# Two products of a hybrid decoder trunk by Strassen's seven-product scheme, with a new table of durations for the instruction planner

## The chip, the cores and the metric

The kernel runs on one core of one Trainium2 chip. The metric is the device time of one execution in microseconds (us), taken as the median of three runs. The profile is of one execution, recorded by the hardware profiler. TensorE is written PE (its weight loads PEld), VectorE is DVE, ScalarE is ACT, GpSimd is POOL, and SyncE, which issues all the transfers here, is SP.

## The reference

Two layers work on 512 tokens of 1024 features, all in float32:

```
h = h + concat(sparse_attention_heads, mlstm_heads) @ w_out      # "mix"
u = rms_norm(h, g_mlp) @ w_ff1                                   # 1024 -> 4096
h = h + square(relu(u)) @ w_ff2                                  # 4096 -> 1024
gate = sigmoid(rms_norm(h, g_ple) @ w_ple_gate + b_ple_gate)     # 1024 -> 1024
h = h + gate * (p_i @ w_ple)
```

The two products that the change touches are the one with `w_ff1` ("ff1") and the one with `w_ple_gate` ("gate").

## The kernel before

**Layout.** The residual stream `h` stays in SBUF as 8 feature blocks of 128 partitions by 512 tokens. A float32 product is made of three passes of float32r matmuls: both operands are split into a leading part `hi` and a remainder `lo`, and `hi*hi`, `hi*lo` and `lo*hi` are added up in one PSUM bank (`mm3`). A weight tile is 128 x 1024 (512 KB). It is loaded into `raw`, ACT writes `hi`, and DVE (in one place POOL may) writes `lo = raw - hi` (`weight`). The block `k` of `h` is scaled by the norm's gain and split by `split_block` in `prep`; POOL adds up the squares for the norm, and `wide_r` turns them into one factor for each token, which is applied to the products' results.

**Order of the MLP.** An output block of ff1 is 8 feature blocks times three passes, 24 matmuls of 128 x 512. `act` takes it out of PSUM with relu and the norm's factor (`s_v`), squares it (`hi` by ACT, `s_vv` by DVE or POOL, and the remainder by DVE). Nine blocks of ff1 stand ahead, then 8 blocks of ff2 (24 matmuls each, added to `h`) and 8 of ff1 take turns, four times in all, the last with no ff1 left. `ple` follows with 8 gate blocks. Two small products of 24 matmuls for the per-layer input (`inputs`, label `filler`) are held for free places on PE.

**What sets the order.** No loop order reaches the chip directly. `Plan` records every instruction, and `schedule` is a list scheduler: an idle engine at once takes the ready instruction with the longest chain of work behind it, using the durations in `cost` and the hops in `lag`. An instruction recorded in forms for two engines goes to the one that takes it first; the engines are asked in the order DVE, ACT, POOL, PE, SP. `issue` writes the result out, so on the chip every engine works through a fixed list. Within a chain (`nc.chain = "mlp"`) the matmuls keep the order in which they were recorded. Buffers come from rooms with a limited number of places (`ROOMS`): 3 for `raw`, 4 for `hi`, 4 for `lo`, 60 for 128 x 512 tiles (`s`), and 6 PSUM banks for products.

All instructions carry the line of `issue` (L381) in the profile, so one goes by tile names.

## Time and profile before

| | |
|---|---|
| time, median of 3 runs | 1372.2 us (1370.88 to 1372.2) |
| the profiled execution's span | 1370.7 us |
| PE busy | 1333.6 us (97%) |
| DVE busy | 887.2 us (65%) |
| ACT busy | 554.8 us (40%) |
| POOL busy | 188.1 us (14%) |
| HBM traffic | 84 GB/s over the span |

The span runs from the first to the last instruction of one execution; the median of the runs shown lies 1.5 us above it, and no other time of the profiled execution itself is given. Busy shares are averages over stages that differ: in the first layer the MLP runs from some 284 to 635 us, and the gate stage, with its two neighbours at the seams, to some 697 us.

### The profile page before, as it was taken

What the parts mean: (1) busy time and instruction counts of PE and PEld (TensorE: products, weight loads), DVE (VectorE), ACT (ScalarE), POOL (GpSimd) and SP (SyncE); (2) the same over time, 40 slices, a digit from 0 to 9 for tenths busy, and PEclk for the clock granted to TensorE, in tenths of its full rate; (3) what the DMA queues carried; (4) which work ended last, traced back from release to release, by engine and by line L of the source; (5) the groups of instructions that cost most, each with busy time, mean ns of one, the idle gap of its engine ahead of it and who ended that gap; (6) DMA issues with size and microseconds to landing.
All of it is one profiled execution on the core that took longest, in us unless ns stands there. A gap on an engine that the chain in (4) does not pass through costs nothing.

```text
span 1370.7 us, 17012 instructions
## 1 busy us (share of the span) xinstructions
PE 1333.6 (97%) x6336; PEld 1096.2 (80%) x6336; DVE 887.2 (65%) x1791; ACT 554.8 (40%) x1106; POOL 188.1 (14%) x151
## 2 busy tenths in 40 slices
PE   7979999999999999999998899999999999999998
PEld 6767889888888888888896778988888888888887
DVE  7989998575354453554859999966743534535454
ACT  4765486332122221234546644844222212222441
POOL 4244200120000000012104341003100000000210
PEclk9989999999999999999999899999999999999999
DMA  5212211333333233333231123103223233323321
GB/s 189 70 55 78 92 32 32 93 92 92 96 95 101 93 92 92 93 100 96 80 90 50 66 83 93 32 21 102 93 93 93 93 97 99 97 93 92 95 83 69
DMA packets 34355, 116.40 MB, mean 85 GB/s; under 512 B 4192, under 2 KB 4704, under 8 KB 34272
## 3 DMA queue, kind: packets, MB, share of 16 engines
q1 hardware_dynamic: 34272, 115.32, 27.4%
q8 instruction: 49, 0.80, 0.2%
q14 instruction: 34, 0.28, 0.1%
HBM read 113.21 MB, written 2.10 MB: 84 GB/s over the span
## 4 chain that ended last, share of the span: by engine, by line
PE 88%; DVE 8%; ACT 2%; issue 1%; DMA 1%; POOL 0%; SPq 0%; ACTq 0%; DVEq 0%; POOLq 0%
PE ps_proj L381 78%; PE ps_sc L381 3%; PE ps_tr L381 3%; DVE s L381 3%; PE ps_po L381 2%; PE ps_pn L381 1%; ACT s L381 1%; DVE s_w L381 1%; DVE wide L381 1%; DVE s_sp L381 1%; DVE m L381 1%; DVE tiny L381 1%; DVE lo L381 0%; POOL s L381 0%; DMA raw<-wa 0%
## 5 line engine op out<-in xcount | busy, mean ns | idle before, releaser
L381 PE MATMUL ps_proj<-s,hi 128*128 128x512 f32 x2960 | 920.1, 393 | 0.4 <-ACT hi L381 0.4
L381 PEld LDWEIGHTS ps_proj<-s,hi 128*128 128x128 f32 x2960 | 554.3, 188 | 127.0 <-issue 1.8
L381 PE MATMUL ps_proj<-s,lo 128*128 128x512 f32 (+1 forms) x1480 | 576.9, 393 | 0.3 <-DVE lo L381 0.3
L381 ACT ACTIVATE hi<-raw 128x1024 fp32r<-128x1024 f32 (+1 forms) x212 | 222.4, 1052 | 646.2 <-PE ps_proj L381 317.3
L381 PEld LDWEIGHTS ps_proj<-s,lo 128*128 128x128 f32 x1480 | 278.2, 188 | 64.1 <-DVE lo L381 0.7
L381 DVE TENSOR_TENSOR lo<-raw,hi 128x1024 fp32r<-128x1024 f32 (+1 forms) x181 | 223.2, 1234 | 33.9 <-ACT hi L381 30.9
L381 DVE TENSOR_TENSOR const<-const,ps_proj 128x512 f32<-128x512 f32 x96 | 66.0, 688 | 224.3 <-PE ps_proj L381 224.3
L381 POOL TENSOR_TENSOR lo<-raw,hi 128x1024 fp32r<-128x1024 f32 x31 | 75.6, 2442 | 531.9 <-ACT hi L381 525.0
L381 DVE SCALAR_TENSOR_TENSOR s_v<-ps_proj,s 128x512 f32<-128x512 f32 x64 | 43.9, 691 | 138.3 <-PE ps_proj L381 138.3
L381 POOL TENSOR_TENSOR s<-s,s 128x512 f32<-128x512 f32 x42 | 68.3, 1626 | 411.5 <-ACT s L381 297.0
L381 PE MATMUL ps_proj<-hi,s 128*128 128x512 f32 (+1 forms) x384 | 112.4, 381 | 7.2 <-ACT hi L381 7.2
L381 PE MATMUL ps_sc<-s,s 128*128 128x384 f32 (+3 forms) x288 | 85.4, 382 | 0.0
L381 PEld LDWEIGHTS ps_proj<-hi,s 128*128 128x128 f32 x384 | 69.3, 194 | 16.3 <-ACT hi L381 7.2
L381 PE MATMUL ps_proj<-lo,s 128*128 128x512 f32 (+1 forms) x192 | 66.5, 385 | 1.9 <-DVE lo L381 1.9
L381 PEld LDWEIGHTS ps_sc<-s,s 128*128 128x128 f32 x288 | 52.5, 195 | 9.4 <-issue 3.1
L381 ACT ACTIVATE s<-ps_tr 128x128 fp32r<-128x128 f32 (+2 forms) x170 | 38.9, 307 | 34.4 <-PE ps_tr L381 34.1
L381 DVE MATCH_REPLACE8 s<-m,s 128x384 f32<-128x384 f32 (+2 forms) x96 | 51.2, 537 | 0.0
L381 DVE TENSOR_TENSOR s<-s_vv,s 128x512 fp32r<-128x512 f32 x64 | 49.2, 773 | 0.2
L381 PE MATMUL ps_po<-at,s_et 128*128 128x64 f32 x320 | 48.9, 254 | 0.0
L381 DVE MAX8 m<-s 128x8 f32<-128x384 f32 (+2 forms) x96 | 48.8, 542 | 0.0
L381 PEld LDWEIGHTS ps_po<-at,s_et 128*128 128x128 f32 x320 | 47.8, 191 | 1.1
L381 DVE SCALAR_TENSOR_TENSOR s<-const,const,s 128x512 fp32r<-128x512 f32 x48 | 39.8, 833 | 11.5 <-ACT s L381 11.4
(133 smaller groups left out, 1105.0 us busy)
## 6 DMA issues: line engine op xcount, KB each, us to landing
raw<-ws SPq DMA_DIRECT2D x204, 512.0 KB, 3.5
raw<-wa SPq DMA_DIRECT2D x8, 336.0 KB, 3.4
const<-xt SPq DMA_DIRECT2D x8, 256.0 KB, 4.7
out<-const SPq DMA_DIRECT2D x7, 256.0 KB, 2.0
s<-pt SPq DMA_DIRECT2D x4, 256.0 KB, 4.1
const<-ct SPq DMA_DIRECT2D x2, 132.0 KB, 4.2
out<-const SPq DMA_DIRECT2D x2, 128.0 KB, 1.7
const<-cf SPq DMA_DIRECT2D x2, 39.0 KB, 2.7
```

The lines of the kernel that those rows point to most:

```text
L381: ins = getattr(getattr(nc, e), method)(*[value(x) for x in args], **{k: value(x) for k, x in kw.items()}).ins
```

## The change

ff1 and the gate product are made by the Winograd form of Strassen's scheme. Two output blocks (rows), the even and odd feature blocks (the inner dimension) and the two halves of the tokens (columns) make a 2 x 2 by 2 x 2 block product, which takes seven block products in place of eight. Each of the seven is 4 feature blocks times three passes of 128 x 256 matmuls. The operands are sums and differences: `seven` makes T1 to T4 from `h` once for each stage, `left` makes S1 to S4 from two weight tiles for every pair of output blocks, and `pair` lets the products add up in three PSUM banks and combines what is left on ACT and DVE. `interleaved` records the products of a pair between those of its neighbour. The host orders the rows of both weights even blocks first (`even_first`), with no other arithmetic there.

Besides, ten blocks of ff1 stand ahead of ff2 where nine did; the first two blocks of ff2 run together, with their last two feature blocks last; the tiles `at` and `vx` become four tiles each in the room `s`, which grows from 60 to 64 places, and `raw` grows from 3 to 4; and `cost` has other numbers.

```diff
             if method == "transpose":
-                return 56.0 if single else 109.0
-            return max(107.0, n / 2.4 + 3) if single else max(214.0, n / 0.6 + 3)
+                return 60.0 if single else 109.0
+            return max(111.0, n * 0.4375 + 7) if single else max(172.0, n * 1.66 + 11)
...
-            return 100 + n * {"tensor_tensor": 2.25, "memset": 0.5, "affine_select": 1.0}.get(method, 1.4)
+            return 100 + n * {"tensor_tensor": 2.4, "memset": 0.8, "affine_select": 1.0}.get(method, 1.4)
...
+    def quads(self, l, gcol):
+        nc = self.nc
+        label = nc.label
+        cf = self.cf[l][0]
+        H = S // 2
+        lower, upper = slice(0, H), slice(H, S)
+        xs, acc = [], None
+        for k in range(KD):
+            nc.label = "prep"
+            x = self.slot([128, S])
+            g = cf[:, gcol + k:gcol + k + 1]
+            nc.scalar.activation(x, self.h[k], AF.Copy, scale=g)
+            nc.label = "squares"
+            sq = self.slot([128, S])
+            nc.scalar.activation(sq, self.h[k], AF.Square)
+            if acc is None:
+                acc = sq
+            else:
+                nacc = self.slot([128, S])
+                nc.gpsimd.tensor_tensor(nacc, acc, sq, op=ALU.add)
+                acc = nacc
+            if k % 2 == 0:
+                b1 = x
+                continue
+            b2 = x
+            nc.label = "prep"
+            xs.append(self.seven(b1, b2))
+        nc.label = label
+        return xs, acc
+    def seven(self, b1, b2):
+        H = S // 2
+        lower, upper = slice(0, H), slice(H, S)
+        t12, t34 = self.slot([128, S]), self.slot([128, S])
+        self.either(t12[:, lower], b1[:, upper], b1[:, lower], ALU.subtract)
+        self.either(t34[:, lower], b2[:, upper], b1[:, upper], ALU.subtract)
+        self.either(t12[:, upper], b2[:, upper], t12[:, lower], ALU.subtract)
+        self.either(t34[:, upper], b2[:, lower], t12[:, upper], ALU.subtract)
+        out = {}
+        mixed = self.slot([128, S], F32R)
+        self.split(b1[:, lower], mixed[:, lower], mixed[:, upper])
+        out["B11"] = (mixed[:, lower], mixed[:, upper])
+        for names, src in ((("B21", "B22"), b2), (("T1", "T2"), t12), (("T3", "T4"), t34)):
+            hi, lo = self.slot([128, S], F32R), self.slot([128, S], F32R)
+            self.split(src, hi, lo)
+            out[names[0]], out[names[1]] = (hi[:, lower], lo[:, lower]), (hi[:, upper], lo[:, upper])
+        return out
+    def either(self, out, a, b, op):
+        nc = self.nc
+        return nc.add([(e, "tensor_tensor", (out, a, b), {"op": op}) for e in ("vector", "gpsimd")])
+    def split(self, src, hi, lo):
+        nc = self.nc
+        nc.scalar.activation(hi, src, AF.Copy)
+        nc.vector.tensor_tensor(lo, src, hi.bitcast(F32), op=ALU.subtract)
+    def left(self, l, i):
+        nc = self.nc
+        a, b = slice(0, 512), slice(512, 1024)
+        r1, r2 = self.slot([128, 1024], F32, "raw"), self.slot([128, 1024], F32, "raw")
+        nc.sync.dma_start(r1, self.ap["ws"][l, i])
+        nc.sync.dma_start(r2, self.ap["ws"][l, i + 1])
+        out = {}
+        def halves(src, names):
+            hi, lo = self.slot([128, 1024], F32R, "hi"), self.slot([128, 1024], F32R, "lo")
+            self.split(src, hi, lo)
+            for name, c in zip(names, (a, b)):
+                out[name] = (hi[:, c], lo[:, c])
+        halves(r1, ("A11", "A12"))
+        s1 = self.slot([128, 512])
+        self.either(s1, r2[:, a], r2[:, b], ALU.add)
+        hi, lo = self.slot([128, 512], F32R), self.slot([128, 512], F32R)
+        self.split(s1, hi, lo)
+        out["S1"] = (hi, lo)
+        self.either(r2[:, a], r1[:, a], r2[:, a], ALU.subtract)
+        self.either(r1[:, a], s1, r1[:, a], ALU.subtract)
+        self.either(r1[:, b], r1[:, b], r1[:, a], ALU.subtract)
+        halves(r1, ("S2", "S4"))
+        halves(r2, ("S3", "A22"))
+        return out
+    def pair(self, l, i, xs, take):
+        nc = self.nc
+        H = S // 2
+        lower, upper = slice(0, H), slice(H, S)
+        w = self.left(l, i)
+        def product(bank, left, right, first=False):
+            steps = [(k, a, b) for k in range(len(xs)) for a, b in ((0, 0), (0, 1), (1, 0))]
+            for n, (k, a, b) in enumerate(steps):
+                nc.tensor.matmul(bank[:, 0:H], w[left][a][:, k * 128:(k + 1) * 128], xs[k][right][b],
+                                 start=first and n == 0, stop=n == len(steps) - 1, skip_group_check=True)
+        u0, u1 = self.slot([128, S]), self.slot([128, S])
+        x, z = self.psum("proj"), self.psum("proj")
+        product(z, "A12", "B21", True)
+        nc.scalar.activation(u0[:, lower], z[:, 0:H], AF.Copy)
+        product(x, "A11", "B11", True)
+        nc.vector.tensor_tensor(u0[:, lower], u0[:, lower], x[:, 0:H], op=ALU.add)
+        yield
+        y = self.psum("proj")
+        product(y, "S1", "T1", True)
+        nc.scalar.activation(u1[:, upper], y[:, 0:H], AF.Copy)
+        product(x, "S2", "T2")
+        nc.scalar.activation(u0[:, upper], x[:, 0:H], AF.Copy)
+        yield
+        product(x, "S3", "T3")
+        nc.vector.tensor_tensor(u1[:, upper], u1[:, upper], x[:, 0:H], op=ALU.add)
+        yield
+        product(y, "S4", "B22")
+        nc.vector.tensor_tensor(u0[:, upper], u0[:, upper], y[:, 0:H], op=ALU.add)
+        product(x, "A22", "T4")
+        take(0, u0, u1, x)
+        yield
+    def interleaved(self, parts):
+        last = None
+        for p in parts:
+            next(p)
+            if last:
+                next(last)
+            next(p)
+            if last:
+                next(last)
+            last = p
+        next(last)
+        next(last)
...
+    def blocks(self, ws, xs, t=slice(0, S), late=1):
         pss = [self.psum("proj") for _ in ws]
-        steps = [(i, k) for i in range(len(ws)) for k in range(KD - 1)] + [(i, KD - 1) for i in range(len(ws))]
+        early = KD - late
+        steps = [(i, k) for i in range(len(ws)) for k in range(early)] \
+            + [(i, k) for i in range(len(ws)) for k in range(early, KD)]
...
-        xs, acc = self.prep(l, C_MLP)
+        xs, acc = self.quads(l, C_MLP)
...
...
+        H = S // 2
+        lower, upper = slice(0, H), slice(H, S)
+        def act(i):
+            def take(n, u0, u1, x):
+                if "r" not in state:
+                    state["r"] = self.wide_r(acc, D)
+                r = state["r"]
+                nc.vector.scalar_tensor_tensor(u0, u0, 0.0, r, op0=ALU.max, op1=ALU.mult)
+                nc.vector.scalar_tensor_tensor(u1[:, lower], x[:, 0:H], 0.0, r[:, lower], op0=ALU.max, op1=ALU.mult)
+                nc.vector.scalar_tensor_tensor(u1[:, upper], u1[:, upper], 0.0, r[:, upper], op0=ALU.max, op1=ALU.mult)
+                for j, v in ((i, u0), (i + 1, u1)):
+                    hi, lo = self.slot([128, S], F32R), self.slot([128, S], F32R)
+                    nc.scalar.activation(hi, v, AF.Square)
+                    self.either(v, v, v, ALU.mult)
+                    nc.vector.tensor_tensor(lo, v, hi.bitcast(F32), op=ALU.subtract)
+                    fs[j] = (hi, lo)
+            return take
+        def ff1(i, n):
+            self.interleaved(self.pair(l, W_FF1 + j, xs, act(j)) for j in range(i, i + n, 2))
         def ff2(c):
-            for n in range(KD):
-                ps, = self.blocks([self.wtile(l, W_FF2 + KD * c + n)], [fs[KD * c + k] for k in range(KD)])
-                nc.vector.tensor_tensor(self.h[n], self.h[n], ps, op=ALU.add)
-                if c == NFF - 1 and n == 0:
+            for n0, cnt in ((0, 2),) + tuple((n, 1) for n in range(2, KD)):
+                ws = [self.wtile(l, W_FF2 + KD * c + n0 + j) for j in range(cnt)]
+                pss = self.blocks(ws, [fs[KD * c + k] for k in range(KD)], late=2)
+                for n, ps in enumerate(pss, n0):
+                    nc.vector.tensor_tensor(self.h[n], self.h[n], ps, op=ALU.add)
+                if c == NFF - 1 and n0 == 0:
                     nc.hold, nc.chain = nc.ops[-1], None
                     self.inputs(l, 1, raws)
                     nc.hold, nc.chain, nc.label = None, "mlp", "mlp"
-        ff1(0, 2)
-        for i in range(2, KD + 1):
-            ff1(i)
+        ff1(0, KD + 2)
         for c in range(NFF):
             ff2(c)
-            for i in range(KD * (c + 1) + 1, min(KD * (c + 2) + 1, KD * NFF)):
-                ff1(i)
+            i = KD * (c + 1) + 2
+            if i < KD * NFF:
+                ff1(i, min(KD, KD * NFF - i))
         nc.chain = None
     def ple(self, l):
...
-        xs, acc = self.prep(l, C_PLE)
+        xs, acc = self.quads(l, C_PLE)
         nc.chain = "mlp"
...
+        state = {}
+        H = S // 2
+        lower, upper = slice(0, H), slice(H, S)
+        def act(n):
+            def end(n, c, u):
+                th, z = self.slot([128, S]), self.slot([128, S])
+                nc.scalar.activation(th[:, c], u[:, c], AF.Tanh, scale=0.5, bias=hb[:, n:n + 1])
+                nc.vector.scalar_tensor_tensor(z[:, c], th[:, c], 1.0, self.pw[l][n][:, c], op0=ALU.add, op1=ALU.mult)
+                nc.vector.tensor_tensor(self.h[n][:, c], self.h[n][:, c], z[:, c], op=ALU.add)
+                if l == L - 1:
+                    nc.sync.dma_start(self.ap["out"][n][:, c], self.h[n][:, c])
+            def take(_, u0, u1, x):
+                if "r" not in state:
+                    state["r"] = self.wide_r(acc, D)
+                r = state["r"]
+                nc.vector.tensor_tensor(u0, u0, r, op=ALU.mult)
+                end(n, slice(0, S), u0)
+                nc.vector.tensor_tensor(u1[:, upper], u1[:, upper], r[:, upper], op=ALU.mult)
+                nc.vector.tensor_tensor(u1[:, lower], x[:, 0:H], r[:, lower], op=ALU.mult)
+                for c in (upper, lower) if l == L - 1 and n == KD - 2 else (slice(0, S),):
+                    end(n + 1, c, u1)
+            return take
+        self.interleaved(self.pair(l, W_GATE + n, xs, act(n)) for n in range(0, KD, 2))
...
-ROOMS = {"s": 60, "raw": 3, "hi": 4, "lo": 4, "at": 1, "vx": 1, "tiny": 48, "wide": 16, "m8": 4, "ps": 8}
+ROOMS = {"s": 64, "raw": 4, "hi": 4, "lo": 4, "tiny": 48, "wide": 16, "m8": 4, "ps": 8}
...
+def even_first(w):
+    l, k, n = w.shape
+    return w.reshape(l, k // 256, 2, 128, n).transpose(0, 2, 1, 3, 4).reshape(l, k, n)
...
```

## Rows read from the trace of the kernel before

**Rows 1.** The page, part 1: the span, and each engine's busy time.

```profile
span 1370.7 us, 17012 instructions
PE 1333.6 (97%) x6336; PEld 1096.2 (80%) x6336; DVE 887.2 (65%) x1791; ACT 554.8 (40%) x1106; POOL 188.1 (14%) x151
```

**Rows 2.** The page, part 4: shares of the chain that ended last.

```profile
PE 88%; DVE 8%; ACT 2%; issue 1%; DMA 1%; POOL 0%; SPq 0%; ACTq 0%; DVEq 0%; POOLq 0%
```

**Rows 3.** Windows: stretch, busy us and instructions by engine, granted clock, DMA.

```profile
core 0: us, PE busy (x) PEld busy (x) DVE busy (x) ACT busy (x) POOL busy (x), PEclk, DMA share, GB/s
24.10:235.70 211.60, 199.87 (x1120) 167.56 (x1121) 195.13 (x613) 131.31 (x366) 52.57 (x43) 0.97 0.21 64
...
261.50:339.60 78.10, 78.10 (x338) 63.20 (x337) 51.94 (x65) 28.13 (x38) 15.17 (x10) 1.00 0.31 95
339.60:384.00 44.40, 44.40 (x193) 36.00 (x192) 16.50 (x18) 9.08 (x9) 0.00 (x0) 1.00 0.30 93
384.00:428.30 44.30, 44.30 (x193) 35.92 (x192) 23.75 (x30) 12.13 (x15) 0.00 (x0) 1.00 0.31 97
634.60:697.00 62.40, 62.40 (x270) 50.53 (x270) 44.71 (x57) 31.72 (x46) 11.28 (x8) 1.00 0.28 82
1309.60:1365.70 56.10, 56.09 (x266) 46.40 (x265) 32.85 (x45) 17.95 (x26) 1.81 (x1) 1.00 0.21 71
```

**Rows 4.** Timeline of PE in the last gate block: start us, us, instruction.

```profile
1359.85 0.40 PE L381 MATMUL ps_proj<-s,hi 128*128 128x256 f32 x2
...
1365.41 0.28 PE L381 MATMUL ps_proj<-s,lo 128*128 128x256 f32 x1
```

**Rows 5.** The tile ps_proj, 1359.8 to 1365.7 us: count, ns min/median/max.

```profile
L381 PEld LDWEIGHTS ps_proj<-s,hi x32: 187/188/192, 1359.6 to 1365.2; 128*128 128x128 f32 x32
```

**Rows 6.** Timeline of DVE: one block of ff1, and a half-width operation.

```profile
307.19 0.69 DVE L381 TENSOR_TENSOR s_vv<-s_v 128x512 f32<-128x512 f32 x1
307.80 1.22 DVE L381 TENSOR_TENSOR lo<-raw,hi 128x1024 fp32r<-128x1024 f32 x1
308.94 0.68 DVE L381 TENSOR_TENSOR s<-s_vv,s 128x512 fp32r<-128x512 f32 x1
...
1362.89 0.42 DVE L381 TENSOR_TENSOR s<-ps_proj,s 128x256 f32<-128x256 f32 x1
```

**Rows 7.** Groups of ACT by form: count, busy us, mean ns, idle before.

```profile
L381 ACT ACTIVATE hi<-raw 128x1024 fp32r<-128x1024 f32 x204 | 216.3, 1063 | 637.4 <-PE ps_proj L381 317.3 <-issue 304.4 <-DMA raw<-ws 9.6
L381 ACT ACTIVATE s<-s_v 128x512 fp32r<-128x512 f32 x64 | 39.1, 616 | 0.0
...
L381 ACT ACTIVATE s_idx<-ps_sc 128x256 f32<-128x256 f32 x16 | 6.6, 414 | 0.1
```

**Rows 8.** Timeline of POOL: three additions of 128 x 512.

```profile
263.58 1.83 POOL L381 TENSOR_TENSOR s<-s,s 128x512 f32<-128x512 f32 x1 [39.92 <-ACT s L381]
266.34 1.29 POOL L381 TENSOR_TENSOR s<-s,s 128x512 f32<-128x512 f32 x1 [0.93 <-ACT s L381]
...
665.55 1.61 POOL L381 TENSOR_TENSOR s<-s,s 128x512 f32<-128x512 f32 x1 [26.99 <-ACT s L381]
```

**Rows 9.** Timeline of DVE beside these three.

```profile
263.52 0.75 DVE L381 SCALAR_TENSOR_TENSOR s<-const,const,s 128x512 fp32r<-128x512 f32 x1
...
267.02 0.69 DVE L381 TENSOR_TENSOR const<-const,ps_proj 128x512 f32<-128x512 f32 x1 [0.54 <-PE ps_proj L381]
...
666.04 1.67 DVE L381 TENSOR_TENSOR const<-const,s 128x512 f32<-128x512 f32 x1
```

**Rows 10.** The tile s_v: POOL's squares of it, ns min/median/max.

```profile
L381 POOL TENSOR_TENSOR s_vv<-s_v x6: 1041/1042/2026, 295.2 to 973.6; 128x512 f32<-128x512 f32 x6
```

More of the change, by code (lines that the diff above doesn't have):

```diff
@@ L768, in mix @@
         nc.label = "keys"
-        at = self.slot([128, NTB, GA], tag="at")
+        at = [self.slot([128, GA]) for _ in range(NTB)]
         pss = [self.psum("proj") for _ in range(NTB)]
@@ L778, in mix @@
         for tb in range(NTB):
-            nc.scalar.activation(at[:, tb], pss[tb][:, 0:GA], AF.Copy, scale=r[:, tb:tb + 1])
-        ks = [at[:, tb, 0:192].split(64) for tb in range(NTB)]
+            nc.scalar.activation(at[tb], pss[tb][:, 0:GA], AF.Copy, scale=r[:, tb:tb + 1])
+        ks = [at[tb][:, 0:192].split(64) for tb in range(NTB)]
         wi = self.tiny([128, NTB, 8])
-        nc.vector.tensor_scalar(wi, at[:, :, 320:328], IDX_SCALE, None, op0=ALU.mult)
+        for tb in range(1, NTB):
+            nc.vector.tensor_scalar(wi[:, tb], at[tb][:, 320:328], IDX_SCALE, None, op0=ALU.mult)
         self.headnorm(ks, 3, ct[:, T_K:T_K + 192], True)
@@ L844, in g4 @@
             return self.tiny([128, NTB, 4])
-        def bias4(col):
-            return ct[:, col:col + 4].unsqueeze(1).broadcast_to([128, NTB, 4])
         gi, gf = g4(), g4()
-        nc.vector.tensor_tensor(gi, at[:, :, 328:332], bias4(T_I), op=ALU.add)
-        nc.vector.tensor_tensor(gf, at[:, :, 332:336], bias4(T_F), op=ALU.add)
+        for tb in range(NTB):
+            nc.vector.tensor_tensor(gi[:, tb], at[tb][:, 328:332], ct[:, T_I:T_I + 4], op=ALU.add)
+            nc.vector.tensor_tensor(gf[:, tb], at[tb][:, 332:336], ct[:, T_F:T_F + 4], op=ALU.add)
         nab, z, y, y2, lp, lf = g4(), g4(), g4(), g4(), g4(), g4()
@@ L897, in mix @@
         nc.chain = "rows"
-        vx = self.slot([128, NTB, 4, 129], tag="vx")
-        nc.gpsimd.memset(vx[:, :, :, 128:129], 1.0)
+        vx = [self.slot([128, 4, 129]) for _ in range(NTB)]
+        for tb in range(NTB):
+            nc.gpsimd.memset(vx[tb][:, :, 128:129], 1.0)
         rh = self.tiny([128, NTB])
@@ L1015, in mix @@
                     c = (tb - sb) * 128
-                    nc.tensor.matmul(where(tb), ptile[sb][:, c:c + 128], vx[:, sb, h], start=sb == 0, stop=sb == tb)
+                    nc.tensor.matmul(where(tb), ptile[sb][:, c:c + 128], vx[sb][:, h], start=sb == 0, stop=sb == tb)
             nc.chain = None
@@ L1113, in ff1 @@
-        def ff1(i, n=1):
-            for j, ps in enumerate(self.blocks([self.wtile(l, W_FF1 + i + j) for j in range(n)], xs)):
-                act(i + j, ps)
-        def ff2(c):
-            for n in range(KD):
-                ps, = self.blocks([self.wtile(l, W_FF2 + KD * c + n)], [fs[KD * c + k] for k in range(KD)])
-                nc.vector.tensor_tensor(self.h[n], self.h[n], ps, op=ALU.add)
-                if c == NFF - 1 and n == 0:
+        H = S // 2
+        lower, upper = slice(0, H), slice(H, S)
@@ L1139, in ple @@
         hb = self.cf[l][1]
-        xs, acc = self.prep(l, C_PLE)
+        xs, acc = self.quads(l, C_PLE)
         nc.chain = "mlp"
-        rbc = None
-        for n0, cnt in ((0, 2), (2, 1), (3, 1), (4, 1), (5, 1), (6, 1), (7, 1)):
-            ws = [self.wtile(l, W_GATE + n0 + j) for j in range(cnt)]
-            last = l == L - 1 and n0 == KD - 1
-            for c in (slice(0, S // 2), slice(S // 2, S)) if last else (slice(0, S),):
-                pss = self.blocks(ws, [(hi[:, c], lo[:, c]) for hi, lo in xs], c)
-                for n, ps in enumerate(pss, n0):
-                    if rbc is None:
-                        rbc = self.wide_r(acc, D)
-                    t, th, z = self.slot([128, S]), self.slot([128, S]), self.slot([128, S])
-                    nc.vector.tensor_tensor(t[:, c], ps[:, c], rbc[:, c], op=ALU.mult)
-                    nc.scalar.activation(th[:, c], t[:, c], AF.Tanh, scale=0.5, bias=hb[:, n:n + 1])
-                    nc.vector.scalar_tensor_tensor(z[:, c], th[:, c], 1.0, self.pw[l][n][:, c], op0=ALU.add, op1=ALU.mult)
-                    nc.vector.tensor_tensor(self.h[n][:, c], self.h[n][:, c], z[:, c], op=ALU.add)
-                    if l == L - 1:
-                        nc.sync.dma_start(self.ap["out"][n][:, c], self.h[n][:, c])
@@ L1228, in layout @@
          row_pairs(wmv), row_pairs(wmo), out_pairs(A["w_out"][:, 512:]), out_pairs(A["w_out"][:, :512]),
-         col_blocks(A["w_ff1"])]
+         col_blocks(even_first(A["w_ff1"]))]
         + [col_blocks(wff2[:, c]) for c in range(NFF)]
-        + [row_pairs(wple[:, :, i]) for i in range(2)] + [col_blocks(A["w_ple_gate"])], axis=1)
+        + [row_pairs(wple[:, :, i]) for i in range(2)] + [col_blocks(even_first(A["w_ple_gate"]))], axis=1)
     wa = row_pairs(np.concatenate([wak, wik, wav, wiw, wmi, wmf], -1))
```

16 lines of the change are left out of this document (2 added, 14 removed).

## The prediction

> **What bounds the kernel now.** I first read the page's busy line: PE is busy for 1333.6 of 1370.7 us, and DVE for two thirds [rows 1]. The chain that ended last says the same: 88% of it is PE [rows 2]. Then I cut the span by stage, since the share of DVE is a mean over stages that differ. The windows [rows 3] show the mix (24 to 236 us) with DVE busy for 195 of 212 us, and ff1, ff2 and the gate with PE busy all the time and the clock at 1.00, its level of 2.4 GHz. There DVE is loaded lightly: 16.5 us of 44.4 where ff2 runs, 23.75 of 44.3 where ff1 does. So every matmul saved in these stages is time saved, as long as the room on DVE is enough for what the scheme asks of it. That is the whole question. PE's list is fixed, so a matmul that waits for a late `lo` holds up all behind it, and their readers.
>
> **Price of a matmul.** A stretch of 193 matmuls of 512 columns takes 44.4 us, 0.230 us each [rows 3]. The last gate block runs in halves of the tokens and so shows the new shape: 48 matmuls of 256 columns, first start 1359.85, last 1365.41, 47 steps of 0.118 us [rows 4]. Each of them has a weight load of its own, 0.188 us long, and these overlap [rows 5]. The Trainium skill, TensorE: Matmul & The Clock Gate, "Back-to-back issue gap", has the columns at 2.4 GHz and 2.5 ns, an estimate of 0.109 and 0.216 us: by it the saving below would be 47 us. The trace has both longer, and I go by the trace.
>
> **PE.** A pair of output blocks took 2 x 24 x 0.230 = 11.04 us, and will take 7 x 12 = 84 matmuls x 0.1183 = 9.94 us: 1.10 less. There are 16 pairs of ff1 and 4 of the gate in a layer, 40 in all: 44.2 us.
>
> **DVE for a pair.** From start to next start, a 1024 operation costs 1.14 us (307.80 to 308.94) and a 512 one 0.61 (307.19 to 307.80); a 256 one runs 0.42, less the same 0.08 of overlap 0.34 [rows 6]. Before: two `lo` of 1024 and six of 512, 5.94 us. After, the weights: three `lo` of 1024, one of 512 and four sums of 512, 3.42 + 0.61 + 2.44 = 6.47. The closing of ff1: three additions from PSUM of 256, relu in one of 512 and two of 256, two squares, two remainders: 1.02 + 1.29 + 2.44 = 4.75; that of the gate comes to the same. Sum 11.22, if DVE does all: more than PE's 9.94, and about what the pair took before. So in a long run of pairs DVE becomes the bound.
>
> **What POOL can take.** The four sums and, in ff1, the two squares may go to POOL. It is not free help. Alone, an addition takes POOL 1.29 us, also beside a DVE operation that reads PSUM (266.34, 267.02); beside one that reads two SBUF tiles POOL's took 1.83 (263.58, 263.52), and where POOL was first (665.55) DVE's took 1.67 in place of 0.69 (666.04) [rows 8, 9]: one waits for the other. A square takes POOL 1.04 [rows 10]. So each operation moved spares DVE 0.61 and holds it up for 1.29, except for what falls beside its four PSUM reads (1.36 us a pair; I take half, 0.68). The Trainium skill, SBUF — State Buffer, "SBUF: two separate sides", says it as a rule: an operation of VectorE with two SBUF inputs and one of GpSimd take one port pair as an exclusive lock for the whole instruction. The trace agrees (1.67 for 0.69); if the two engines did not wait for each other, three operations moved would leave a pair 9.4 us and no loss.
>
> How many move is the planner's choice: DVE is asked first, but whatever becomes ready while DVE is busy and POOL idle goes to POOL. The planner's costs hold nothing of the port. I take three of six: D = 11.22 - 1.83 + 3.87 - 0.68 = 12.6 us for a pair. Bounds: none moved 11.2; all six and nothing beside PSUM, 11.22 - 3.66 + 4 x 1.29 + 2 x 1.04 = 14.8.
>
> **Where this is paid.** *Start of the MLP* (out's second half to the end of the first ff1, 261.5 to 339.6): PE does ten blocks in the 78.1 us of nine. DVE has 51.9 [rows 3]; five pairs add 5 x 11.22 - 9 x 2.97 = 29.4; `seven` in place of `prep` adds, for a pair of blocks of `h`, 3.53 - 1.34 = 2.2 (five of 256, three of 512, less two splits), 8.8 in all: 90.1. Some may run behind under ff2: its first 36 matmuls (8.3 us) need none of the last two blocks, and the last pair's closing (3.7) has longer. That leaves 78.1, just PE's; each us of D above 11.2 costs 5 us here. D = 12.6: 7.0 for a layer, 14.0 in all.
>
> *Later runs of four, four and three pairs* have ff2 around them, where DVE idles 28 of 44.4 us [rows 3]. The first pair's weights come ahead and the last closing behind: four pairs need (4 - 10.2 / 11.2) D = 3.09 D = 38.9 us, under PE's 39.8. Nothing is lost, until D passes 12.9.
>
> *Gate.* First layer, 634.6 to 697: DVE 44.7, plus 4 x 5.28 for the pairs, 2.2 for the last of `seven`, less 4.2 for weights made ahead under ff2: 63.8; two of the four sums on POOL add 2.7: 66.5 against 62.4 before, 4.1 lost where PE would gain 4.4. Second layer, 1309.6 to 1365.7: 32.9 + 21.1 + 2.2 - 4.2 + 2.7 = 54.7 against 56.1, 1.4 gained.
>
> *Starts of ff1 and of the gate.* The last block of `h` was needed after 42 matmuls (9.7 us); now after 9 of 256 columns (1.1 us), and it must be scaled and split, some 2.6 us. The 24 filler matmuls (5.5 us) can cover it where the planner keeps them. I take 1 us for each of four starts, 4.0; bounds 0 and 10.
>
> **At nothing.** ACT has 3 x 1.06 + 0.62 + 3 x 0.41 + 2 x 0.62 = 6.3 us a pair [rows 7], beside 9.94; without that cover it would cost nothing until it passed D. Transfers move the same bytes at a DMA share of 0.31 [rows 3]; if they went faster with PE, the share would be 0.34. SP issues weights in the same order, with four `raw` for three. The rest (tiles of `at` and `vx`, more places, the table) reorders the mix, where PE idles some 11 us a layer: nothing, between 8 gained and 8 lost. The end behind the last product, 5 us now, has halves again.
>
> **Sum.** ff1 16 x 2 x 1.10 = 35.4, less 14.0; gate +1.4 - 4.1; starts -4.0: 14.7 less than the span of 1370.7 is 1356.0. The median of the runs stands 1.5 above that span, so **1357 us**.
>
> **Rivals.**
> 1. *DVE hides everything*: the planner leaves the sums on DVE (D = 11.2) and the work ahead and behind covers the rest. Then 35.4, +4.1 - 1.4 for the gate, less the starts: 34 less, 1338; all of the 44.2 would be 1328. For it: 28 us free in each ff2. Against it: 90.1 us of DVE at each start of the MLP.
> 2. *The shared port makes it slower.* POOL takes five of six: D = 11.22 - 3.05 + 6.20 - 0.68 = 13.7. The starts of the MLP lose 25, the runs of four 4 x (42.3 - 39.8) = 10, the gate with three of four sums moved 8.1, the starts 4: 47.1 against 35.4 is 12 slower, 1384; at D = 14.8 some 1420. It decides from D = 13.4, between four and five moved. For it: the planner knows no port, and DVE is busy nearly all the time in its plan too. Against it: it asks DVE first. The page named above bears on this one; by it the lock is total, as I reckon here.
> 3. *PE waits for places*, not for work. Two pairs at once hold three of the four `hi` places each in turn, and S3's part can be made only in the 4.3 us (three products) after S4's is free: 1.06 + 1.14 and three hops, some 3 us. A DVE queue of over 1.3 us there stalls PE; 1.1 us a pair eats all: 1372.
> 4. *The weight load shows*: at one load of 0.188 us per matmul a pair would take 15.8 us, 190 us more. The 48 matmuls at 0.118 [rows 4, 5] speak against it.
>
> **Chances.** Forecast (two to four moved) 0.45; rival 1 0.15; rival 2 0.27; rival 3 0.10; rival 4 0.03. The range leaves out rival 4, the far end of rival 2 and the best of rival 1: 1332 to 1394; the forecast's own is 1340 to 1370. A difference of 0.2% is about what a measurement of this kernel tells from none. Faster: 0.42 of the forecast, rival 1 and a little of rival 3, 0.59; within 0.2%: 0.10; slower: rival 2 and the rest, 0.31.
>
> **What would show it.** Right: matmuls of 256 columns 0.118 us apart; PE without idle in the later runs of ff1; in the first run and the gate PE waiting for DVE `lo`, with DVE busy over 90% there; DVE operations with two SBUF inputs stretched beside POOL's additions; POOL with some 100 to 150 operations in these stages. Wrong: if POOL takes nearly all sums (rival 2), if PE waits evenly in every pair (rival 3), or if DVE is idle at the first run (rival 1).

## The result and the profile after

The changed kernel takes 1468.2 us (median of 4 runs, 1463.0 to 1473.9), the kernel before on the same chip 1372.2: a ratio of 1.070, 95% interval [1.067, 1.073]. The forecast was 1357, the range 1332 to 1394. The profiled execution has a span of 1461.2. The page's parts 1 and 4 and three groups of part 5 (group; count | busy us, mean ns | idle before it):

```profile
span 1461.2 us, 20775 instructions
PE 1336.8 (91%) x7752; PEld 1154.7 (79%) x7752; DVE 1187.7 (81%) x2154; ACT 690.7 (47%) x1368; POOL 409.8 (28%) x307
...
PE 26%; DVE 17%; ACT 2%; issue 2%; DMA 1%; POOL 1%; DVEq 0%; ACTq 0%; POOLq 0%
...
L381 PE MATMUL ps_proj<-s,hi 128*128 128x256 f32 (+1 forms) x3584 | 890.1, 340 | 60.9 <-DVE s L381 42.8
...
L381 POOL TENSOR_TENSOR s<-s 128x512 f32<-128x512 f32 (+1 forms) x60 | 88.8, 1480 | 290.9 <-ACT s L381 290.9
...
L381 POOL TENSOR_TENSOR s<-s,s 128x512 f32<-128x512 f32 (+1 forms) x65 | 94.7, 1468 | 69.6 <-ACT s L381 52.4
```

Against [rows 1, 2]: PE is as long busy as before although its work is 44 us less by the count of matmuls (the busy time also holds what runs at a lower clock, and the ends of matmuls that stand alone), and it waits 42.8 us for DVE's `s` ahead of the first group alone, of which [rows 3] show nothing in ff1, ff2 and the gate; DVE has 300 us more, POOL 222. The chain that ended last is followed back only to 745.76 us here, so its shares add up to 49% of the span, where those of [rows 2] add up to 100%. Of what it covers PE has 26 of 49, about half, and DVE 17; before, PE had 88 of 100 and DVE 8.

The price of a matmul is not what went wrong. PE's timeline in a later run of ff1 (start, us, instruction):

```profile
428.16 0.40 PE L381 MATMUL ps_proj<-s,hi 128*128 128x256 f32 x2
...
434.10 0.28 PE L381 MATMUL ps_proj<-s,lo 128*128 128x256 f32 x1
```

From 428.16 to 434.10 there are 50 steps (two hi and one lo in turn), 0.119 us each, as in [rows 4]. What did go wrong is seen where out's second half hands over to ff1. PE's timeline there, and windows of 3 us (columns as in [rows 3]):

```profile
293.74 0.28 PE L381 MATMUL ps_proj<-s,lo 128*128 128x256 f32 x1
298.54 0.58 PE L381 MATMUL ps_proj<-s,hi 128*128 128x256 f32 x1 [4.52 <-ACT s L381]
302.08 0.58 PE L381 MATMUL ps_proj<-s,hi 128*128 128x256 f32 x1 [2.96 <-DVE s L381]
302.46 0.42 PE L381 MATMUL ps_proj<-s,lo 128*128 128x256 f32 x1
305.87 0.58 PE L381 MATMUL ps_proj<-s,hi 128*128 128x256 f32 x1 [2.99 <-ACT s L381]
308.47 0.58 PE L381 MATMUL ps_proj<-s,hi 128*128 128x256 f32 x1 [2.02 <-DVE s L381]
...
309.49 0.63 PE L381 MATMUL ps_proj<-s,hi 128*128 128x256 f32 x2
309.91 0.41 PE L381 MATMUL ps_proj<-s,lo 128*128 128x256 f32 x1
```

```profile
294.00:297.00 3.00, 0.02 (x1) 0.00 (x0) 3.00 (x5) 1.99 (x3) 1.40 (x1) 0.94 0.00 0
297.00:300.00 3.00, 0.58 (x1) 0.29 (x1) 3.00 (x3) 1.46 (x3) 2.65 (x3) 0.50 0.00 0
300.00:303.00 3.00, 0.80 (x2) 0.50 (x2) 2.81 (x5) 1.54 (x4) 2.84 (x3) 0.50 0.37 111
303.00:306.00 3.00, 0.13 (x1) 0.14 (x1) 3.00 (x4) 2.81 (x6) 2.75 (x2) 0.50 0.16 64
306.00:309.00 3.00, 0.98 (x3) 0.69 (x4) 3.00 (x6) 2.29 (x4) 1.10 (x2) 0.50 0.00 0
309.00:312.00 3.00, 3.00 (x14) 2.81 (x13) 2.11 (x4) 0.71 (x2) 0.00 (x0) 0.50 0.09 15
```

Of the 15.6 us from 293.7 to 309.3 PE stands idle for 12.5, in the four waits shown, while DVE is busy nearly all the time and POOL beside it. The granted clock falls to 0.50, the level of 1.2 GHz, once PE stands still, and is still there when PE works again: at 309.5 a matmul of 256 columns takes 0.21 us in place of 0.118.

For the whole span I cut each trace into stretches, from one set of additions to `h` on DVE to the next (the eighth addition of ff2 or of out's half ends one), and subtracted the length that the stretch has in the kernel before. In us:

```
kernel                  span   first  out 2, first  later   gate and    out 2, first  later  last
                               mix    run, ff2      runs    second mix  run, ff2      runs   gate
before                1370.7  255.9   117.3         261.4   297.7       117.1         260.2  61.1
after                 1461.2  +15.2   +30.0          +4.3   +21.9       +24.0          -2.7  -2.2
e1 table alone        1419.5  +25.2    +0.2          -0.4   +23.8        +0.2           0.0  -0.1
e8 scheme, sums DVE   1393.5   -1.5   +20.4         -10.4   +11.0       +21.6         -13.0  -5.3
e5 and the tiles      1399.9  +11.7   +20.4         -16.5    +9.7       +16.2         -10.7  -1.5
e6 and sums on POOL   1409.3  +12.2   +19.1          -9.4    +8.6       +19.8          -9.6  -2.1
e14 and all on POOL   1423.4  +12.1   +23.6          -6.7   +10.0       +23.1          -7.9  -1.5
e16 and the new table 1464.8  +19.7   +26.6          -0.7   +26.9       +25.3          -2.3  -1.5
e13 later runs alone  1341.6   -1.7    -6.1          -4.0    -4.2        -5.4          -2.2  -5.5
```

Read the columns with care: the stretches end with additions on DVE, and the planner moves PE's work across these ends. In e8's first layer the stretch of the first run holds 474 matmuls of 256 columns, where its five pairs have 420: 54 belong to the next pair, some 6 us at 0.118. And the 48 matmuls of 512 columns of the first layer's two small products, 11 us at 0.230, stand behind 634.6 us in the kernel before, at the start of the gate; in e8, 47 of them run ahead of the end of the last ff2 (24 up to 561 us, the others just before that end), in the column of the later runs. So a stage's gain or loss can't be read from its column alone. What PE loses depends less on the ends. It is its idle time, and its busy time x (1 - granted clock), here added up from windows of 2.5 us, in us (in e8 the first start of ff1 is 263 to 387 us, that of the first gate 638 to 674, and "behind the first gate" is 674 to 744):

```
                        first   two starts    starts of the  behind the   later runs    second  end
                        mix     of ff1        two gates      first gate                 mix
before                  26.2     0.0   0.0     0.0   0.0      0.4          0.0   0.0    13.4    5.0
e8 scheme, sums DVE     24.8    14.2  15.6     6.9   5.1     19.0          3.1   0.0    13.6    8.3
after                   35.5    21.4  20.7     5.3   3.2     12.0         19.1   5.8    23.7    8.7
```

### The profile page after: what moved, and what is told of

Read it like the earlier page. It is cut to its first block, busy times and chain, and to the rows that moved or that the text cites. A ratio compares the mean times of both kernels' runs of the same rounds, so it can differ in the third digit from the quotient of the medians.

```text
span 1461.2 us, 20775 instructions
## 1 busy us (share of the span) xinstructions
PE 1336.8 (91%) x7752; PEld 1154.7 (79%) x7752; DVE 1187.7 (81%) x2154; ACT 690.7 (47%) x1368; POOL 409.8 (28%) x307
## 5 line engine op out<-in xcount | busy, mean ns | idle before, releaser
L381 PE MATMUL ps_proj<-s,hi 128*128 128x256 f32 (+1 forms) x3584 | 890.1, 340 | 60.9 <-DVE s L381 42.8
L381 PE MATMUL ps_proj<-s,lo 128*128 128x256 f32 (+1 forms) x1792 | 603.1, 338 | 10.8 <-DVE lo L381 10.7
L381 PEld LDWEIGHTS ps_proj<-s,lo 128*128 128x128 f32 x1792 | 343.9, 192 | 51.0 <-DVE lo L381 14.2
L381 DVE TENSOR_TENSOR lo<-raw,hi 128x1024 fp32r<-128x1024 f32 (+1 forms) x223 | 299.0, 1343 | 28.1 <-ACT hi L381 28.0
L381 DVE TENSOR_TENSOR s<-s,s 128x512 fp32r<-128x512 f32 (+4 forms) x237 | 228.8, 986 | 2.6 <-ACT s L381 1.8
L381 POOL TENSOR_TENSOR s<-s 128x512 f32<-128x512 f32 (+1 forms) x60 | 88.8, 1480 | 290.9 <-ACT s L381 290.9
L381 ACT ACTIVATE s<-s 128x512 fp32r<-128x512 f32 (+2 forms) x182 | 108.5, 607 | 121.0 <-DVE s L381 88.9
L381 POOL TENSOR_TENSOR s<-s,s 128x512 f32<-128x512 f32 (+1 forms) x65 | 94.7, 1468 | 69.6 <-ACT s L381 52.4
L381 PE MATMUL ps_sc<-s,s 128*128 128x256 f32 (+3 forms) x288 | 83.1, 382 | 8.2 <-ACT s_idx L381 3.7
L381 DVE SCALAR_TENSOR_TENSOR s<-s,s 128x512 f32<-128x512 f32 (+1 forms) x93 | 65.7, 712 | 1.6
```

The costliest lines, as they stand in the source:

```text
L381: ins = getattr(getattr(nc, e), method)(*[value(x) for x in args], **{k: value(x) for k, x in kw.items()}).ins
```

## The experiments

Times are medians; "before" in them was 1371.4 to 1372.6 throughout.

**Parts that have nothing to do with the products.** e1 is the kernel before with the new table alone.

```
-                return 56.0 if single else 109.0
-            return max(107.0, n / 2.4 + 3) if single else max(214.0, n / 0.6 + 3)
+                return 60.0 if single else 109.0
+            return max(111.0, n * 0.4375 + 7) if single else max(172.0, n * 1.66 + 11)
```

(and POOL's two figures.)

> The kernel before with the new table of durations alone; plain products, old tiles and places. The changed kernel loses 15.2 us in each layer between the gate (or the start) and the end of the first half of the output product, where no product was changed. Theory A (the table reorders the mix badly): that loss is here, 30 us for both layers, the time is near 1402. Theory B (the tiles of at and vx and the places do it): the mix keeps its length and the time is 1372, within 4 us.

1419.8 us, 1.035 [1.033, 1.036]: 48 us from a few numbers that no instruction reads. All of it lies in the two mixes, +25.2 and +23.8, ff1 and ff2 within 0.3. The window of e1's first mix stands against the first of [rows 3]:

```profile
24.10:260.90 236.80, 214.79 (x1137) 174.73 (x1137) 210.95 (x624) 130.21 (x361) 53.17 (x41) 0.95 0.19 59
```

PE idles for 22.0 us in place of 11.7, DVE for 25.9 in place of 16.5, and the clock is 0.95 in place of 0.97: the same work in an order that leaves more gaps.

e2 is the kernel before with the tiles of `at` and `vx` and the places of the changed one (`"s": 64, "raw": 4`, four tiles each for one), old table.

> The kernel before with at and vx in four tiles each, 64 places for 128x512 tiles and 4 for raw; old table, plain products. Theory A (the table): 1372, within 4 us. Theory B (tiles and places): 30 us longer, 1402. If both this and the table alone lose some 15, the two share the loss.

1385.1, 1.010 [1.008, 1.011]; +11.9 in the first mix, nothing elsewhere.

e3 is the changed kernel with the old table.

> The changed kernel with the old table. Theory A: it gives the 30 us of the mix back, 1438; if the table is also worse for the interleaved pairs, more. Theory B: the mix stays as long, 1468. Rival: the old table is further from the chip in the new stages (its 512 matmul is 216 ns where the trace has 230), and the start of the MLP loses more, so the sum is over 1468.

1452.8, 1.058 [1.056, 1.060]. Only 15.4 of e1's 48 come back.

**Which engine does the scheme's extra work.** e4: the changed kernel with all of `either` on DVE, and 61, 5 and 5 places for `s`, `hi` and `lo`.

```
-    def either(self, out, a, b, op):
+    def either(self, out, a, b, op, engines=("vector", "gpsimd")):
...
-        self.either(s1, r2[:, a], r2[:, b], ALU.add)
+        self.either(s1, r2[:, a], r2[:, b], ALU.add, ("vector",))
```

(and the same in its other calls.)

> The changed kernel with all sums of weights, the sums of the activations and the squares of ff1 on DVE alone; so that the planner finds an order, hi and lo have 5 places and the 128x512 tiles 61. Port theory: DVE needs 11.2 us for a pair in place of the 13 and more of the changed kernel, its operations keep their lengths (0.69 and 1.23), and out's second half, the starts of the MLP and the gates get shorter by 25 to 40 us together. Rival, places: PE waits for hi and the tiles, whoever adds; then it is not shorter, and longer by what 3 places less cost in the mix. Rival, DVE alone is too slow: the start of the MLP (90 us of DVE by my count against 78 of PE) gets longer by 10 us in each layer.

1423.3, 1.037 [1.036, 1.039], 45 less than the changed kernel, though its first mix, with other places, is 31.3 over before. In the second layer its later runs are 4.2, 5.4 and 2.6 shorter than before.

Since table and places confuse these, the next four take the old table, and fix the order in which the four `hi` places are taken (S2 and S4 ahead of S3 and A22, and the next pair's A11 behind S2). e5:

```
-        halves(r1, ("S2", "S4"))
-        halves(r2, ("S3", "A22"))
+        halves(r1, ("S2", "S4"), "S3")
+        halves(r2, ("S3", "A22"), "S2")
...
-                    self.either(v, v, v, ALU.mult)
+                    nc.scalar.activation(v, v, AF.Square)
```

with `either` on DVE alone in `left` and `seven`. The last name says behind whose split the new one waits; S2 and S4 wait behind the S3 of the last pair.

> The changed kernel's tiles and places, with the old table of durations, and with nothing of the scheme's extra work on POOL: the four sums of weights of each pair and the five sums of each pair of blocks of h on DVE, the squares on ACT. The order in which the hi places are taken is fixed by hand (S2 and S4 ahead of S3). It differs from e6 only in where the sums of weights run, and from e8 only in the mix. If the port shared by DVE and POOL is what the changed kernel loses in ff1, this one keeps the gain of PE wherever DVE has room: DVE's work for a pair is 11.2 - 1.2 (two squares) = 10.0 us, just PE's 9.9, so the runs of four pairs are some 4 us shorter than before, the first run some 5 us longer (five sums of h for each pair of blocks stay), the first mix 12 longer as with the tiles alone: 1372 + 12 - 4 = about 1380, between 1370 and 1392. If instead PE waits for hi and lo places, whatever engine makes the sums, the runs of ff1 stay as long as in the changed kernel with the old table, and it comes to 1430 or more.

1401.4, 1.021 [1.020, 1.023]: 9 above the expected range. Runs of four pairs are 4.1 to 4.8 us shorter, as expected, the starts some 16 to 20 longer, not 5.

e6, `left` on either engine again:

> As e5, but the sums of weights may go to POOL again, where the planner puts some 73 of 128 in ff1 and 23 of 32 in the gate; squares on ACT and the sums of h on DVE, as in e5. The shared port: a sum on POOL spares DVE 0.61 us and holds it up for about 1.29, so 96 of them cost 96 x 0.68 = 65 us of DVE, of which the stages that are bound by DVE (the first run of ff1, the gates) show a third to a half: 20 to 35 us slower than e5. If POOL's help is worth more than its hold on the port, it is faster than e5. If places are the limit, the two are the same within 5 us.

1411.2, 1.029 [1.027, 1.030]: 9.8 above e5, half of the least expected. POOL made 96 of the 160 sums. The same group of DVE in e5 and in e6 (count | busy us, mean ns):

```profile
L381 DVE TENSOR_TENSOR s<-s,s 128x512 fp32r<-128x512 f32 x164 | 114.2, 714 | 10.1 <-ACT s L381 9.7
```

```profile
L381 DVE TENSOR_TENSOR s<-s,s 128x512 fp32r<-128x512 f32 x164 | 145.2, 898 | 7.2 <-ACT s L381 6.1
```

In the changed kernel this mean is 1053. The stretching is there, 31.0 us in this group from e5 to e6, but most of it falls where PE does not wait: the kernel is 9.8 us longer.

e7, the squares on DVE in place of ACT:

> As e5, but the 64 squares on DVE instead of ACT: 1.2 us more of DVE for a pair of ff1 (11.2 in place of 10.0), so DVE is over PE's 9.9. If DVE's length for a pair sets the pace, some 5 us more in each first run of ff1 and 0 to 3 in each later run of four: 8 to 20 us slower than e5. If DVE has room, no difference.

1408.8, 1.027 [1.025, 1.028]: 7.4 above e5, just under the expected 8 to 20.

e8, e5 with `mix`, its tiles and places (58 of `s`) as before:

> As e5, but with the mix, its tiles for at and vx and the rest of the places as in the kernel before (58 places of 128x512 and four raw). If the first mix's 12 us of the changed tiles are independent of the scheme, it is e5 less 12, near 1368, between 1358 and 1378: the only version so far that can beat the kernel before. If the mix is longer because PE's or DVE's work behind it has changed, it stays where e5 is.

1395.3, 1.017 [1.015, 1.018]. That is above its range too. The first mix is back at its old length, but of its 12 us only 6.0 stay gained: the stretches behind it are longer than in e5, which may be the 58 places; that was not tried.

e11, e6 with the squares on either engine:

> e6 with the squares as in the changed kernel, on DVE or POOL, where the planner puts some 50 of 64 on POOL; nothing else differs from e6. The changed kernel with the old table is at 1453, e6 at 1411: three things lie between them, the squares, the sums of h on either engine and the fixed order of the hi places. If the port makes the squares dear, a square on POOL holds up DVE and the lo behind it: ff1's later runs lose 3 to 10 us each as in the changed kernel's first layer, 15 to 35 us slower than e6. If they run beside DVE's reads of PSUM, the same as e6 within 4 us.

1420.6, 1.035 [1.033, 1.037]: 9.4 over e6, below the expected 15 to 35. Against e7, which has the same six operations all on DVE, POOL's share of the six costs 11.8.

e14, e11 with `seven` on either engine too:

> e11 with the sums of h on DVE or POOL at the planner's choice, as in the changed kernel; it then differs from the changed kernel with the old table (e3) only in the fixed order of the hi places. If POOL's sums of h at the starts are dear through the port, most of the 32 us between e11 and e3: 1440 to 1453. If the order in which S2, S4 and S3, A22 take the hi places is what e3 lacked, within 5 us of e11: 1416 to 1426.

1425.2, 1.039 [1.037, 1.041]. Only 4.6 more; the other 27.6 us up to e3 are the order of the `hi` places. In e3 two later runs of the first layer were 5.7 and 10.1 us longer than before, in e14 2.9 and 0.8 shorter. ACT's `hi` waited for PE there for 66.6 us in e3 (413 to 600 us) and for 45.3 in e14 (409 to 590), which fits a wait for `hi` places.

e16, the changed kernel with that order alone:

> The changed kernel, its new table and POOL's part as they are, with the hi places taken in the fixed order of e5 to e14 alone. If the wait for places is a loss of its own, what e14 gained on e3, 28 us: 1440 (1432 to 1448). If the new table already keeps the planner from that order, as its shorter later runs in the first layer suggest (2.9 and 2.7 us over before, where e3 has 5.7 and 10.1), some 10 us or less: 1456 to 1470.

1466.7, 1.068 [1.066, 1.070]: 1.5, nothing. That would fit a planner that, with the new table, does not fall into that order; the order itself was not read. From e14 to e16 only the table differs: 41.5 us. With the order left to the planner, from e3 to the changed kernel, the same table costs 15.4. So the two losses overlap, and how 43 us split between them depends on which is taken first: 27.6 for the order and 15.4 for the table, or 41.5 for the table and 1.5 for the order.

**What holds PE up at the starts.** e9, e8 with the first pair opened side by side:

```
+            three = (z, "A12", "B21"), (x, "A11", "B11"), (y, "S1", "T1")
+            for k in range(len(xs)):
+                for bank, left, right in three:
```

> e8, with the first pair of each MLP and each gate opened in another order: the three products that need no other (A12 x B21, A11 x B11, S1 x T1) go side by side through the pairs of blocks of h, so the last pair of h is needed after 27 matmuls of 256 columns and not after 9. If the stall at the starts (PE idle for some 11 us behind out's second half, then at a granted clock of 0.5) is the wait for the last pair of h alone, 18 matmuls at 0.118 go into it, 2.1 us at full clock and up to 4 at half, at four starts: 8 to 16 us faster than e8. If DVE is short of time as a whole there (it is busy without a gap from 275 to 325 us in e5), what PE does earlier it waits for later: within 3 us of e8.

1392.2, 1.015 [1.014, 1.016]: 3.2 less. The last pair of `h` alone is not it.

e10, e8 with `t12, t34 = b1, b2` and the four subtractions of `seven` left out:

> e8 without the four sums of h in seven: the products that take T1 to T4 get the halves of the two blocks themselves, so the output is not the product; all splits, products and closings stay. It takes 16 operations of 256 columns (0.34 us each, 5.4 us of DVE) out of each of the four starts, and three of them out of the chain behind the last block of h. If DVE is short of time at the starts, each start is 5 to 8 us shorter (the clock comes back earlier too): 20 to 32 us faster than e8. If only the chain behind the last block counts, 3 x 0.6 = 2 us each, 8 in all. If the stall has another cause (places, the weights of the first pair), within 3 us of e8.

1381.0, 1.006 [1.005, 1.008]: 14.3 less, between the two theories, 0.66 us for each of DVE's 21.6. e15 leaves out the four sums of `left` too:

> e10 with the four sums of weights of each pair left out too (the products take the halves of the two blocks of weights as they are, so the output is not the product): 4 x 0.61 = 2.4 us less of DVE for each of 40 pairs, all splits, products and closings as they were. If DVE's time is what is short at the starts, the first run's five pairs and the gates' four gain at the rate of e10 (14.3 us for 21.6 of DVE, 0.66): 18 x 2.44 x 0.66 = 29 us less than e10, 1352 (1340 to 1362), near the 1328 that PE alone would allow. If it is the length of the chain behind the last block of h or the places, within 6 us of e10's 1381.

1353.4, 0.986 [0.985, 0.988]: 27.7 less again, where DVE's theory said 29. PE executes the same 7752 matmuls in e8, e10 and e15. What PE loses at the four starts (idle time and clock, as in the table above) falls from 41.8 us in e8 to 25.9 in e10 and 13.4 in e15, and behind the first gate from 19.0 to 17.8 and 7.8. So DVE's work is what PE waits for there, but not at the starts alone.

**Only part of the scheme.** e12, the kernel before with the last gate alone by the scheme:

> The kernel before, with ff1 and the first layer's gate as they are there, and only the second layer's gate by the scheme, all its sums on DVE. In e8 the stretch from the last ff2 to the end was 5.3 us shorter than before, in e4 4.3, for four pairs x 1.1 = 4.4 of PE. If that stands alone, 1372 - 5 = 1367 (1364 to 1370). If it was there only since the stretch ahead took over part of its work, or the start of the gate stalls as that of ff1 does, 1371 to 1378.

1375.7, 1.002 [1.001, 1.003]. Its last run is 2.0 us longer and the gate 1.9: the eight blocks' sums have no room ahead of it. e8's 5.3 there is not the gate's own: its last stretch holds 5 matmuls of the small products, where the kernel before and e12 have 36, 7 us more at 0.230.

e13 leaves the first eight blocks of ff1 (`FIRST` is 8) and the gates plain:

```
-        for i in range(2, KD + 1):
+        for i in range(2, FIRST):
             ff1(i)
+            if i in (2, 4, 6, 7):
+                nc.hold = nc.ops[nc.tail["mlp"]]
+                qs.append(self.again(l, C_MLP, 2 * len(qs), xs))
...
+                self.interleaved(self.pair(l, W_FF1 + j, qs, act2(j)) for j in range(i, min(i + KD, KD * NFF), 2))
```

> The kernel before (its mix, its table, plain gates), with the first eight blocks of ff1 plain and only the other 24, twelve pairs a layer, by the scheme. The sums of h are made from h again, behind matmuls of the first run and ahead of the first ff2's additions, so they are off the start; sums on DVE, squares of these pairs on ACT, four raw and 58 places of 128x512. If the loss sits at the starts and PE's gain in the later runs is real, 2 x 12 x 1.10 = 26.5 us less than before: 1346 (1340 to 1356). If the later runs were shorter in e5 and e8 only since work had moved out of them, or DVE is late for the sums of h and the first pairs behind ff2, 1370 or more.

1343.7, 0.979 [0.978, 0.981]: 28.2 us less than before, where 26.5 was worked out, and the only version with all of the scheme's arithmetic that beats it. Windows of it: from out's second half through the first run, and two later runs with the ff2 behind each.

```profile
261.50:339.60 78.10, 78.10 (x341) 63.50 (x340) 60.54 (x88) 37.97 (x56) 20.99 (x13) 1.00 0.31 95
...
365.40:449.70 84.30, 84.30 (x530) 75.88 (x529) 56.11 (x80) 36.27 (x53) 0.00 (x0) 1.00 0.32 100
449.70:534.00 84.30, 84.30 (x530) 75.89 (x530) 55.52 (x78) 36.31 (x53) 2.40 (x1) 1.00 0.36 107
```

PE is busy throughout at clock 1.00, and DVE has a third of the time free. The stretch of four pairs and an ff2 takes 84.3 us, 4.6 less than before; 4 x 1.10 is 4.4.

## Why the prediction was wrong

A chain of kernels gives the 96 us; behind its first step, which has the whole scheme with four `raw` and 58 places, each differs in one thing from the one ahead: before 1372.0; scheme with sums on DVE and squares on ACT +23.3 (e8); tiles and places +6.0 (e5); sums of weights on POOL +9.8 (e6); squares on POOL +9.4 (e11); sums of `h` on POOL +4.6 (e14); new table +41.5 (e16); order of the `hi` places +1.5 (the last two in this order; the other way they are 15.4 and 27.6).

**PE's price and saving: right.** 0.119 measured for 0.118, and e13 gives the saving in full. In e8 it is there too: PE is idle for 87.4 us in all (before 37.1), and busy time x (1 - granted clock), in windows of 2.5 us, comes to 23.2 (before 7.9). Idle and clock cost 65.6 us more and the span grew by 22.8, so PE's work shrank by 42.8, of 44.2 forecast.

**"Starts of ff1 and of the gate: I take 1 us for each of four starts, 4.0; bounds 0 and 10", and the start of the MLP as one sum: the step that failed by most.** With all six operations on DVE and none on POOL, the prediction's own arithmetic gave 1338 (its rival 1). e7 is that case, 1408.8, or 1402.7 without the tiles' 6.0: 65 us off. In e8, where DVE has still less to do, the four starts cost 14.2, 15.6, 6.9 and 5.1 us of idle time and clock, 41.8 where 4.0 stood. The sum over 261.5 to 339.6 set 90 us of DVE against 78 of PE and let 12 run behind. But the deficit does not lie at the end of that stretch, it lies ahead of its first product: eight additions to `h` (4.9), four times `seven` (14.1), A11, A12 and S1 of two pairs (4.7) are 23.7 us of DVE, by the prediction's durations, that must end before PE can run on, in the 22.2 us of out's second half, and the last parts can't begin before the last `h`. And they take longer than that, since POOL is at work in this place even where it makes none of the scheme's sums: it adds up the squares for the norm. Two windows of e8, and two additions of POOL with the operation of DVE that runs into each (of 512 and of 256 columns, 0.61 and 0.34 by the prediction):

```profile
275.00:281.00 6.00, 2.90 (x15) 2.08 (x13) 6.00 (x11) 4.39 (x8) 2.26 (x2) 1.00 0.00 0
281.00:297.00 16.00, 10.59 (x61) 10.07 (x62) 15.19 (x25) 8.22 (x14) 1.76 (x2) 0.68 0.10 33
```

```profile
262.03 1.87 POOL L381 TENSOR_TENSOR s<-s,s 128x512 f32<-128x512 f32 x1 [39.98 <-ACT s L381]
280.08 1.40 POOL L381 TENSOR_TENSOR s<-s,s 128x512 f32<-128x512 f32 x1 [0.87 <-ACT s L381]
```

```profile
262.67 1.78 DVE L381 TENSOR_TENSOR raw<-raw,raw 128x512 f32<-128x512 f32 x1
280.29 1.48 DVE L381 TENSOR_TENSOR s<-s 128x256 f32<-128x256 f32 x1
```

DVE works there without a gap from 259.99 to 290.14, 30.1 us, on operations that come to 23.4 by the prediction's durations, so some 6.7 us are stretch, by this estimate; seven such additions of POOL fall into it. No run takes them away. PE stood idle for 8.5 us in these two windows, and then ran at half the clock. A loss ahead of the first product can't be made up under ff2. e13, which takes the sums out of this place, gives the time back (PE has no idle time at its starts), and e15, which takes them away, most of it. The cover that the prediction named, 24 filler matmuls, was there at e8's first gate and did not suffice: these 24 end at 643.9 us, and after the gate's first three matmuls PE waits 3.8 us; the kernel before has all 48 in that place. The clock was no term of the sum at all, and a third handover was priced at nothing: behind the first layer's gate the second mix needs all of `h`, and in e8 PE idles 12.4 us from 690 to 710, where the kernel before goes on without a gap; with the clock this place costs 18.6 us more than before.

**"At nothing, between 8 gained and 8 lost": the second.** The table alone costs 48 us in the kernel before; in the changed one it costs 15.4, or 41.5 once the order of the `hi` places is fixed. The tiles cost 6 to 13. PE's 11 us of idle in a mix were taken for the measure of what an order can lose; an order can also add idle, and with it clock.

**POOL: mechanism right, size near.** 1.9 of four sums and 1.75 of two squares of an ff1 pair moved (75 of 160 and 56 of 64 in the trace), 3.6 of six where three were taken. The sum had 7.0 for each start of the MLP and 2.7 for each gate, 19.4; e7 to e11 measures 11.8, and the sums of `h`, which had not been priced on POOL, add 4.6. The lock of [rows 8, 9] stretches DVE as said (1053 ns for 714 without POOL's sums), but PE pays for it only where DVE is what it waits for. The rule that the prediction weighed here (the Trainium skill, SBUF — State Buffer, "SBUF: two separate sides") agrees with these means; it does not say whether PE waits for the engine that is held up. Rival 2's time, 1384, was passed by things that are not in it.

**Later runs "lose nothing": right where the scheme's sums and squares are kept off POOL** (nothing lost in e5 and e13, 3.1 us in one layer of e8), and not in the changed kernel, where PE's idle time and clock cost 19.1 us in the first layer's later runs and 5.8 in the second's, and nothing before. POOL, the table and the starts overlap there; how these share it was not taken apart. **Gate:** 4.1 lost and 1.4 gained were forecast; the first, from the last addition of ff2 to the second mix's first transposes, took 69.3 us for 62.4, the second 2.2 less; both hold other amounts of the small products than before, so neither is the gate's own. In e12, where they stay in their place, the second gate alone by the scheme is 1.9 us longer.

**Rival 3, waiting for places:** with the old table the order in which the places are taken costs 27.6 us (e3 to e14), with the new one 1.5. **Rival 4** did not come: matmuls of 256 columns follow at 0.119.

Left open: which line of the table turns the mix, and why the changed kernel suffers from it in ff1 too.

## What to carry to other kernels

A sum of an engine's work over a stretch says only that it can fit; where the next stage's first product needs all of it, set the work that must end before that product against the time before that product. Put a scheme that trades PE for DVE where DVE idles and where its operands can be made early (e13: 28 us gained), not at handovers (e8, which has it there too: 23 lost). And a scheduler's table is part of the program: time it alone, as e1 does, before it goes out with another change.

## What was not expected of the hardware

After PE stood still for a few us the granted clock was 0.50, and it was still there while PE worked again, up to 312 us in the windows above. So a stall costs more than its idle time: at that start 3.6 us more, on 17.8 idle. DVE's operations with two SBUF inputs took 1.05 us on the mean in the changed kernel, where they take 0.71 without POOL's sums. POOL's squares of 128 x 512 took 1.50 on the mean of 56, where the six of the kernel before took 1.37 (their median, which the prediction used, is 1.04 and the longest 2.03, [rows 10]). Both engines pay, and it is the engine that PE waits for that decides whether anybody notices.
